# Hybrid decoder trunk: memory, x and norm weights also laid out features first, and the first layer's transposes replaced by loads

## The chip, the cores and the metric

The kernel runs on one core of a Trainium2 chip. The metric is the device time of one execution in microseconds (us). The kernel before was timed three times on the chip: 2645.34, 2647.21 and 2647.49 us, so its median is 2647.21 us. One more execution was taken with the hardware profiler; all views of the trace below are of that one.

## The reference

Four decoder layers act on x (256 rows of 2048 features, f32), with a memory of 256 rows of 2048 features. Cut to what matters here:

```python
mem_n = _rmsnorm(mem, mem_norm)
for i in range(DEPTH):                     # 4 layers
    h = _rmsnorm(x, norm_in[i])
    self_out, mq, gate = mixer_i(h)        # one of three causal mixers
    mem_out = _memory_attention(mq, mem_n @ w_mem_kv[i])
    y = concatenate([self_out, mem_out]) * silu(gate)
    x = x + y @ w_out[i]
return _rmsnorm(x, final_norm)
```

with `_rmsnorm(x, g) = x / sqrt(mean(x*x) + 1e-6) * g`. A product such as `mem_n @ w` sums over the 2048 features, so TensorE wants both operands with features on the partitions. The factor `1/sqrt(mean)` belongs to a row and can be applied to the product afterwards; the weight g belongs to a feature and is applied to the operand.

## The kernel before, in words

**Arithmetic.** Every f32 operand is split into two float32r parts, high and low: ScalarE copies the source into the high part (`split`, L60), VectorE subtracts it from the source to give the low part (L64). A product is the sum of high times high, high times low and low times high.

**Products.** `rows_by` (L222 on) makes 256 rows by up to 512 columns. It walks over the k tiles (128 features each) of a weight matrix in pairs. `stage` (L207) loads a pair (512 KB) on SyncE's queue (SP) into one of five buffers `wr`; `parts_of` splits one k tile into `wh` and `wl` (three buffers each); six matmuls of 128x512 follow (L234 to L236, for each half of the rows high times high, high times low, low times high). `columns_by` (L239 on) makes the transposed product, 256 columns at a time, four k tiles to a load (also 512 KB), each k tile with two pairs of matmuls (L253, 512 wide, and L255, 256 wide). The accumulators of both (`acc`) share four PSUM buffers, two to a call.

**Features first.** `to_features` (L182 on) takes 128 rows of 512 features, transposes four 128x128 blocks on TensorE into a PSUM tile (L186), multiplies by the norm weight of each feature on VectorE (L188) and splits the result (L60, L64). The norm weights come as rows (`vectors`, L78), are transposed on TensorE (`vectors_T`, L91) and lie in `gvec` with a feature on each partition.

**Order.** The program first prepares the memory for all four layers (`memory`, L307 on): for each of four chunks of 512 features it loads the memory's rows (`mrow`), makes `mT` by `to_features` and squares the rows for the mean (`square_sum`, L197: one ScalarE instruction and one that reads the accumulator). Then come a reduction, `rsqrt_mean` (twelve small VectorE instructions, L157 to L169) and `spread`, which lays the row factor along the columns through two small matmuls (L178). Then for layer i and half p_: one `rows_by` product "mv" (values), its scaling and store, and two `columns_by` products "mk" (keys, heads h). After the first mv product `late_constants` loads x and the other norm weights on SP, and after the first two mk products the four chunks of x go through `to_features` for layer 0 (`Norm.chunk`). The layers follow.

**What sets the order.** The kernel is traced in the order above and then planned: a list scheduler puts each engine's instructions into a fixed queue, ahead of their place in the program where its own timeline finds them ready and the engine free. `tc.keep_in_program_order` pins an instruction behind the one traced before it on its engine. A tile tag with `bufs=n` has n buffers, and a new tile waits for one to be released. Tag `pq` (five buffers of 4 KB a partition) holds the memory rows here, later the keys and queries. In the trace the planner has put the four loads of x, which the program has after the first product, at 9.96 us on SP's queue, and the transposes of x between the matmuls from 31.31 us on.

Of the kernel before, what the change touches and what calls it, by code (L numbers as in the profile page):

```python
# [8 lines left out]
F32 = mybir.dt.float32  # L9
# [22 lines left out]
def kernel(ctx: ExitStack, tc: tile.TileContext, a: dict, out: bass.AP,  # L32
# [39 lines left out]
    rows = cst.tile([P, P], F32, name="rows")  # L72
    mrow = []

    def vectors(src, o, n, eng):
        if len(src.shape) == 2:
            src = src.rearrange("l d -> (l d)")
        eng.dma_start(rows[o:o + n, :], src.rearrange("(r c) -> r c", c=P))  # L78

    def memory_rows(c):  # L80
        q = act.tile([P, 2, 512], F32, name="mrow", tag="pq", bufs=PQ)
        mrow.append(q)
        for t in range(2):
            eng = nc.scalar if t else nc.sync
            eng.dma_start(q[:, t, :], min_[t][:, c * 512:(c + 1) * 512])

    gvec = cst.tile([P, P], F32, name="gvec")

    def vectors_T(o, n):
        gp = misc("gp")  # L90
        nc.tensor.transpose(gp[:, :n], rows[o:o + n, :], ident[o:o + n, o:o + n])  # L91
        nc.vector.tensor_copy(gvec[:, o:o + n], gp[:, :n])
# [89 lines left out]
    def to_features(dst, t, src, gcol, n=4):  # L182
# [9 lines left out]
        g3 = xg[:, :n * P].rearrange("p (j c) -> p j c", j=n)  # L192
        split(dst[:, 0, :n, sl], dst[:, 1, :n, sl], g3)

    def square_sum(col, src):
        junk = tmp("junk")
        nc.scalar.activation(junk[:, :src.shape[-1]], src, AF.Square, accum_out=col)  # L197
# [21 lines left out]
        split(wh[:, :n], wl[:, :n], wr[:, c0:c0 + n])  # L219
        return wh, wl  # L220

    def rows_by(xt, kts, w, k0, cols, name):  # L222

        acc = [ps.tile([P, 512], F32, name=f"acc_{name}{t}", tag="acc", bufs=4) for t in range(2)]
        for s in range(0, kts, ST):
            m = min(ST, kts - s)
            wr, n = stage(w, k0 + s, m, cols)
            for k in range(m):
                wh, wl = parts_of(wr, k * n, n)
                q = xt[(s + k) // 4]  # L230
                for t in range(2):
                    xh, xl = (q[:, v, (s + k) % 4, t * P:(t + 1) * P] for v in range(2))
                    first, last = s + k == 0, s + k == kts - 1
                    nc.tensor.matmul(acc[t][:, :n], xh, wh[:, :n], start=first, stop=False)  # L234
                    nc.tensor.matmul(acc[t][:, :n], xh, wl[:, :n], start=False, stop=False)  # L235
                    nc.tensor.matmul(acc[t][:, :n], xl, wh[:, :n], start=False, stop=last)  # L236
# [37 lines left out]
    class Norm:  # L274
# [32 lines left out]
    def memory():  # L307
# [4 lines left out]
        mT = []  # L312
        for c in range(4):
            if c < 2:
                memory_rows(c + 2)
            q = act.tile([P, 2, 4, S], F32R, name="mT", tag=f"big{c}")
            mT.append(q)
            for t in range(2):
                to_features(q, t, mrow[c][:, t, :], c * 4)
                square_sum(mss[:, t * 4 + c:t * 4 + c + 1], mrow[c][:, t, :])  # L320
        s2 = small("ms2", 2)
        nc.vector.tensor_reduce(s2, mss.rearrange("p (t c) -> p t c", t=2), AX.X, OP.add)
        rsqrt_mean(mrstd, s2, D)
        nc.vector.tensor_scalar(m16, mrstd, 0.0625, None, op0=OP.mult)
        spread(mbc, m16)
        copies = [(v, g) for v in range(2) for g in range(4)]
        for i in range(depth):
            w = a["w_mem_kv"][i]
            for p_ in range(2):
                acc = rows_by(mT, 16, w, 0, (MEMW + p_ * 512, 512), "mv")  # L330
                v = [act.tile([P, 2, 512], F32R, name="mv", tag="aux", bufs=AUX) for z in range(2)]
                for t in range(2):
                    sc = mrstd[:, t:t + 1]
                    copy_act(v[0][:, t, :], acc[t], scale=sc)
                    nc.vector.scalar_tensor_tensor(v[1][:, t, :], acc[t], sc, f32(v[0])[:, t, :],
                                                   op0=OP.mult, op1=OP.subtract)
                for z in range(2):
                    nc.gpsimd.dma_start(mv[i][p_][:, z], v[z])
                if i == p_ == 0:
                    late_constants()  # L340
                for h in (2 * p_, 2 * p_ + 1):
                    acc = columns_by(mT, 16, w, 0, (h * 256, 256), "mk")
                    kT = act.tile([P, 2, 2, S], F32R, name="mkT", tag="pq", bufs=PQ)
                    for j in range(2):
                        z = total(acc[j])
                        zs = wk.tile([P, S], F32, name="zs", tag="z", bufs=3)
                        nc.vector.tensor_mul(zs, z, mbc)
                        split(kT[:, 0, j, :], kT[:, 1, j, :], zs)
                    nc.gpsimd.dma_start(mkT[i][h], kT)
                step = 2 * i + p_  # L350
                if step == 0:
                    for c in range(4):
# [500 lines left out]
def _constants():  # L853
# [18 lines left out]
            "c_cos": np.concatenate([c, c], 1), "c_sin": np.concatenate([-s, s], 1)}  # L872


_INS = ["x", "mem", "norm_in", "final_norm", "mem_norm", "rel_bias", "w_in_a", "a_q_norm", "w_uq",
        "a_kv_norm", "w_ukv", "w_in_b", "w_in_c", "c_sinks", "w_mem_kv", "w_out"]


# [19 lines left out]
```

## Time and profile before

| | before |
|---|---|
| median of 3 timed runs | 2647.21 us |
| the profiled execution's own time | 2644.4 us |
| its span, first to last instruction | 2642.5 us |
| TensorE matmul busy | 2614.7 us (99%) |
| VectorE busy | 1900.3 us (72%) |
| ScalarE busy | 1627.2 us (62%) |
| DMA moved | 507.51 MB, mean 192 GB/s |
| mean granted TensorE clock | 0.998 |

The profile page lists busy time by engine (PE is TensorE's matmuls, PEld its weight loads, DVE VectorE, ACT ScalarE, POOL GpSimd, SP SyncE), the chain of work that ended last, and groups of instructions by line. In a timeline row the first number is the start, the second the time that the merged instructions take, then engine, line, operation, output<-inputs, shapes and count; in brackets stands how long the engine sat idle before it and for whom. In a row of groups stand the busy sum in us, the mean ns of one instruction, and the idle time before. In a row of DMA issues stand the count, the size of one and the median us from issue to landing.

### The profile page before, as it was taken

What the parts mean: (1) busy time and instruction counts of PE and PEld (TensorE: products, weight loads), DVE (VectorE), ACT (ScalarE), POOL (GpSimd) and SP (SyncE); (2) the same over time, 40 slices, a digit from 0 to 9 for tenths busy, and PEclk for the clock granted to TensorE, in tenths of its full rate; (3) what the DMA queues carried; (4) which work ended last, traced back from release to release, by engine and by line L of the source; (5) the groups of instructions that cost most, each with busy time, mean ns of one, the idle gap of its engine ahead of it and who ended that gap; (6) DMA issues with size and microseconds to landing.
All of it is one profiled execution on the core that took longest, in us unless ns stands there. A gap on an engine that the chain in (4) does not pass through costs nothing.

```text
span 2642.5 us, 43005 instructions
## 1 busy us (share of the span) xinstructions
PE 2614.7 (99%) x14623; PEld 2268.1 (86%) x14623; DVE 1900.3 (72%) x4174; ACT 1627.2 (62%) x3460; POOL 57.8 (2%) x102
## 2 busy tenths in 40 slices
PE   8999999999999999999999999999999999999998
PEld 7788888888888888888888888888888888888886
DVE  7566656677777786877777776777778767777767
ACT  6455556566656566666666666666666656665555
POOL 1000000000000000000000000000000000000000
PEclk9999999999999999999999999999999999999999
DMA  7888887565557655555556565555555756655763
GB/s 266 273 269 270 278 262 209 160 191 161 171 164 216 191 191 168 170 184 173 172 166 193 189 191 177 169 175 180 189 166 164 203 163 188 165 170 153 224 184 134
DMA packets 454065, 507.51 MB, mean 192 GB/s; under 512 B 69300, under 2 KB 352180, under 8 KB 452692
## 3 DMA queue, kind: packets, MB, share of 16 engines
q1 hardware_dynamic: 439716, 446.42, 55.5%
q0 software_dynamic: 13120, 56.17, 6.7%
q8 instruction: 115, 1.88, 0.3%
q10 hardware_dynamic: 1008, 2.16, 0.2%
q14 instruction: 106, 0.87, 0.1%
HBM read 485.70 MB, written 31.56 MB: 196 GB/s over the span
## 4 chain that ended last, share of the span: by engine, by line
PE 97%; DMA 2%; DVE 1%; ACT 0%; issue 0%; ACTq 0%; POOLq 0%
PE acc_g L253 14%; PE acc_g L255 7%; PE acc_wo L234 7%; PE acc_wo L235 7%; PE acc_wo L236 7%; PE acc_mq L253 5%; PE acc_mk L253 5%; PE acc_qn L253 3%; PE acc_cq L253 3%; PE acc_mq L255 2%; PE acc_mk L255 2%; PE acc_q L234 2%; PE acc_q L235 2%; PE acc_q L236 2%; PE acc_mv L235 2%; PE acc_mv L234 2%
## 5 line engine op out<-in xcount | busy, mean ns | idle before, releaser
L64 DVE TENSOR_TENSOR wl<-wr,wh 128x512 fp32r<-128x512 f32 (+2 forms) x1776 | 1171.6, 663 | 609.7 <-ACT wh L60 577.7
L60 ACT ACTIVATE wh<-wr 128x512 fp32r<-128x512 f32 (+2 forms) x1776 | 1080.5, 609 | 809.6 <-PE acc_g L253 172.4
L253 PE MATMUL acc_g<-xT,wh 128*128 128x512 f32 x1536 | 518.8, 398 | 0.0
L255 PE MATMUL acc_g<-xT,wl 128*128 128x256 f32 x1536 | 374.2, 282 | 0.0
L255 PEld LDWEIGHTS acc_g<-xT,wl 128*128 128x128 f32 x1536 | 287.5, 189 | 28.0
L235 PE MATMUL acc_wo<-wl,y 128*128 128x512 f32 x768 | 303.6, 395 | 0.8 <-DVE wl L64 0.8
L236 PE MATMUL acc_wo<-wh,y 128*128 128x512 f32 x768 | 298.6, 390 | 0.0
L253 PEld LDWEIGHTS acc_g<-xT,wh 128*128 128x128 f32 x1536 | 265.2, 188 | 36.4
L234 PE MATMUL acc_wo<-wh,y 128*128 128x512 f32 x768 | 240.7, 393 | 0.6 <-ACT wh L60 0.6
L253 PE MATMUL acc_mq<-xT,wh 128*128 128x512 f32 x512 | 173.2, 397 | 0.0
L253 PE MATMUL acc_mk<-mT,wh 128*128 128x512 f32 x512 | 171.4, 397 | 0.0
L235 PEld LDWEIGHTS acc_wo<-wl,y 128*128 128x128 f32 x768 | 144.3, 188 | 29.7 <-DVE wl L64 1.6
L236 PEld LDWEIGHTS acc_wo<-wh,y 128*128 128x128 f32 x768 | 144.3, 188 | 27.9
L234 PEld LDWEIGHTS acc_wo<-wh,y 128*128 128x128 f32 x768 | 141.7, 188 | 28.9 <-ACT wh L60 0.8
L805 DVE TENSOR_TENSOR x<-x,acc_wo 128x512 f32<-128x512 f32 x192 | 126.2, 681 | 12.3 <-PE acc_wo L236 12.1
L253 PE MATMUL acc_qn<-cT,wh 128*128 128x512 f32 x384 | 129.6, 398 | 0.0
L253 PE MATMUL acc_cq<-xT,wh 128*128 128x512 f32 x384 | 127.8, 395 | 0.0
L255 PE MATMUL acc_mq<-xT,wl 128*128 128x256 f32 x512 | 126.5, 285 | 0.0
L255 PE MATMUL acc_mk<-mT,wl 128*128 128x256 f32 x512 | 123.0, 282 | 0.0
L255 PEld LDWEIGHTS acc_mk<-mT,wl 128*128 128x128 f32 x512 | 96.6, 189 | 10.8
L235 PE MATMUL acc_q<-wl,xT 128*128 128x512 f32 x256 | 102.4, 400 | 0.0
L235 PE MATMUL acc_mv<-wl,mT 128*128 128x512 f32 x256 | 100.8, 394 | 0.3 <-DVE wl L64 0.3
(284 smaller groups left out, 4533.9 us busy)
## 6 DMA issues: line engine op xcount, KB each, us to landing
wr<-in_w_out_dram SPq DMA_DIRECT2D x192, 512.0 KB, 3.7
wr<-in_w_in_a_dram SPq DMA_DIRECT2D x176, 512.0 KB, 3.8
wr<-in_w_mem_kv_dram SPq DMA_DIRECT2D x128, 512.0 KB, 4.7
wr<-in_w_in_b_dram SPq DMA_DIRECT2D x112, 512.0 KB, 3.4
wr<-in_w_in_c_dram SPq DMA_DIRECT2D x104, 512.0 KB, 3.5
wr<-in_w_uq_dram SPq DMA_DIRECT2D x288, 128.0 KB, 2.7
tab<-flat POOLq DMA_DIRECT2D x8, 1536.0 KB, 11.0
wr<-in_w_in_a_dram SPq DMA_DIRECT2D x32, 288.0 KB, 3.2
```

Source lines behind the costliest of these rows:

```text
L60: nc.scalar.activation(o, i, AF.Copy, scale=scale)
L64: nc.vector.tensor_sub(lo, src, f32(hi))
L234: nc.tensor.matmul(acc[t][:, :n], xh, wh[:, :n], start=first, stop=False)
L235: nc.tensor.matmul(acc[t][:, :n], xh, wl[:, :n], start=False, stop=False)
L236: nc.tensor.matmul(acc[t][:, :n], xl, wh[:, :n], start=False, stop=last)
L253: nc.tensor.matmul(acc[j], wh[:, o:o + P], q[:, :, kt % 4, :], start=first, stop=False)
L255: nc.tensor.matmul(acc[j][:, 0, :], wl[:, o:o + P], q[:, 0, kt % 4, :], start=False, stop=last)
L805: nc.vector.tensor_add(xs, xs, acc[t])
```

## The change

Three more arrays are given: `l_mem` and `l_x` (memory and x with a feature on each partition: 128 partitions x 16 blocks x 256 rows) and `l_norms` (all norm weights, one feature on each partition, 64 KB). `gvec` is loaded from `l_norms` by the first DMA on ScalarE's queue. The norm rows, their transposes and the copies are gone.

- The memory's features come in four chunks `ft` (two DMAs of 256 KB each, tag `pq`) on ScalarE's queue: two chunks ahead of everything, the other two asked for inside the first product. The first product calls `prepare(c)` before every fourth k tile, which makes chunk c of `mT` by `weighted_parts`: for each k tile ScalarE copies 128x256 with the weight as scale, and VectorE subtracts (one scalar_tensor_tensor of 128x256).
- The memory's rows are still loaded for the squares, all eight loads pinned on SP behind the weight loads of the first mk product (`row_scales`). The first mv product's scaling (`values`) now comes after that mk product and after `row_scales`.
- `late_constants` moves behind both mk products of the first step, and its four loads of x are pinned.
- For layer 0, `Norm.chunk` loads `l_x` (two DMAs of 256 KB for each of four chunks, on SP, not pinned, tag `pq`) and uses `weighted_parts` in place of `to_features`; the squares are still taken from x's rows. Layers 1 to 3 go on with `to_features`.

```diff
+    gvec = cst.tile([P, P], F32, name="gvec")
+    nc.scalar.dma_start(gvec, a["l_norms"])
+    def features(src, c, eng):
+        q = act.tile([P, 4, S], F32, name="ft", tag="pq", bufs=PQ)
+        for k in range(0, 4, 2):
+            eng.dma_start(q[:, k:k + 2, :], src[:, 4 * c + k:4 * c + k + 2, :])
+        return q
+    mft = [features(a["l_mem"], c, nc.scalar) for c in range(2)]
     ident = cst.tile([P, P], F32, name="ident")
     nc.scalar.dma_start(ident, a["c_ident"])
-    memory_rows(0)
-    vectors(a["mem_norm"], 0, 16, nc.gpsimd)
-    memory_rows(1)
-    vectors_T(0, 16)
...
-                nc.sync.dma_start(x[t][:, cs], xin[t][:, cs])
-        vectors(a["norm_in"], 64, 64, nc.sync)
-        vectors(a["a_q_norm"], 32, 24, nc.sync)
-        vectors(a["a_kv_norm"], 56, 8, nc.sync)
-        vectors_T(64, 64)
-        vectors_T(32, 32)
+                tc.keep_in_program_order(nc.sync.dma_start(x[t][:, cs], xin[t][:, cs]))
...
+    def weighted_parts(dst, src, gcol):
+        for k in range(4):
+            g = gvec[:, gcol + k:gcol + k + 1]
+            copy_act(dst[:, 0, k, :], src[:, k, :], scale=g)
+            nc.vector.scalar_tensor_tensor(dst[:, 1, k, :], src[:, k, :], g, f32(dst)[:, 0, k, :],
+                                           op0=OP.mult, op1=OP.subtract)
...
             wr, n = stage(w, k0 + s, m, cols)
+            if prepare is not None and s % 4 == 0:
+                prepare(s // 4)
...
+            if self.layer == 0:
+                weighted_parts(q, features(a["l_x"], c, nc.sync), 64 + c * 4)
             for t in range(2):
                 src = x[t][:, c * 512:(c + 1) * 512]
-                to_features(q, t, src, 64 + self.layer * 16 + c * 4)
+                if self.layer:
+                    to_features(q, t, src, 64 + self.layer * 16 + c * 4)
...
+        def prepare(c):
             if c < 2:
-                memory_rows(c + 2)
+                mft.append(features(a["l_mem"], c + 2, nc.scalar))
+            weighted_parts(mT[c], mft[c], c * 4)
+        def row_scales():
+            for c in range(4):
+                q = act.tile([P, 2, 512], F32, name="mrow", tag="pq", bufs=PQ)
+                for t in range(2):
+                    tc.keep_in_program_order(
+                        nc.sync.dma_start(q[:, t, :], min_[t][:, c * 512:(c + 1) * 512]))
+                    square_sum(mss[:, t * 4 + c:t * 4 + c + 1], q[:, t, :])
...
-                acc = rows_by(mT, 16, w, 0, (MEMW + p_ * 512, 512), "mv")
+                begins = i == p_ == 0
+                acc = rows_by(mT, 16, w, 0, (MEMW + p_ * 512, 512), "mv", prepare if begins else None)
+                if not begins:
+                    values(i, p_, acc)
+                for h in (2 * p_, 2 * p_ + 1):
+                    acck = columns_by(mT, 16, w, 0, (h * 256, 256), "mk")
+                    if begins and h == 0:
+                        row_scales()
+                        values(i, p_, acc)
+                    keys(i, h, acck)
+                if begins:
                     late_constants()
```

More of the change, by code (lines that the diff above doesn't have):

```diff
@@ L311, in memory @@
         mss = small("mss", 8, bufs=2)
-        mT = []
-        for c in range(4):
+        mT = [act.tile([P, 2, 4, S], F32R, name="mT", tag=f"big{c}") for c in range(4)]
+        def prepare(c):
             if c < 2:
-                memory_rows(c + 2)
-            q = act.tile([P, 2, 4, S], F32R, name="mT", tag=f"big{c}")
-            mT.append(q)
-            for t in range(2):
-                to_features(q, t, mrow[c][:, t, :], c * 4)
-                square_sum(mss[:, t * 4 + c:t * 4 + c + 1], mrow[c][:, t, :])
@@ new lines, in values @@
+        def values(i, p_, acc):
+            v = [act.tile([P, 2, 512], F32R, name="mv", tag="aux", bufs=AUX) for z in range(2)]
+            for t in range(2):
+                sc = mrstd[:, t:t + 1]
+                copy_act(v[0][:, t, :], acc[t], scale=sc)
+                nc.vector.scalar_tensor_tensor(v[1][:, t, :], acc[t], sc, f32(v[0])[:, t, :],
+                                               op0=OP.mult, op1=OP.subtract)
+            for z in range(2):
+                nc.gpsimd.dma_start(mv[i][p_][:, z], v[z])
@@ L326, in memory, with keys @@
+        def keys(i, h, acc):
+            kT = act.tile([P, 2, 2, S], F32R, name="mkT", tag="pq", bufs=PQ)
+            for j in range(2):
+                z = total(acc[j])
+                zs = wk.tile([P, S], F32, name="zs", tag="z", bufs=3)
+                nc.vector.tensor_mul(zs, z, mbc)
+                split(kT[:, 0, j, :], kT[:, 1, j, :], zs)
+            nc.gpsimd.dma_start(mkT[i][h], kT)
         copies = [(v, g) for v in range(2) for g in range(4)]
@@ L887 @@
     arrays, args = {}, {}
-    for name, v in [(n, inputs[n]) for n in _INS] + list(_constants().items()):
+    for name, v in ([(n, inputs[n]) for n in _INS] + list(_laid_out(inputs).items())
+                    + list(_constants().items())):
         v = _np.ascontiguousarray(v)
```

60 lines of the change are left out of this document (17 added, 43 removed).

## The prediction

> **What bounds the kernel now.** I read the page first: the busy sums, then the chain that ended last.
>
> ```profile
> PE 2614.7 (99%) x14623; PEld 2268.1 (86%) x14623; DVE 1900.3 (72%) x4174; ACT 1627.2 (62%) x3460; POOL 57.8 (2%) x102
> PE 97%; DMA 2%; DVE 1%; ACT 0%; issue 0%; ACTq 0%; POOLq 0%
> ```
>
> TensorE is the bound nearly everywhere: 97% of the chain is its matmuls. Work taken off it counts in full, and other engines' work counts only where TensorE waits. So next came the timeline of TensorE for the start, and two rows of the table by stage (us, PE, PEld, DVE, ACT, POOL busy, clock, DMA share, GB/s).
>
> ```profile
> 7.62 0.28 PE L91 MATMUL gp<-ident,rows 16*128 16x16 f32 x1 [7.62 <-DMA rows<-in_mem_norm_dram]
> 7.83 6.17 PE L186 MATMUL tp<-ident,mrow 128*128 128x128 f32 x32
> 14.31 0.73 PE L234 MATMUL acc_mv<-wh,mT 128*128 128x512 f32 x2 [0.31 <-ACT wh L60]
> ...
> 10.00:15.00 5.00, 4.69 (x26) 4.06 (x24) 5.00 (x9) 5.00 (x13) 0.00 (x0) 1.00 1.05 389
> 14.30:40.00 25.70, 25.35 (x121) 20.48 (x121) 22.54 (x52) 18.47 (x40) 0.00 (x0) 1.00 0.78 276
> ```
>
> The first product starts at 14.31: 7.62 us wait for a load of norm weights, then 32 transposes. From 14.30 to 40.00 TensorE idles 25.70 - 25.35 = 0.35 us. So the opening is as good as a product that starts at 14.66 and never waits. That opening, and the transposes of x later, are all that the change can win.
>
> **The change: transposes of x.** In the matmul timeline ten of them stand between two products, and the norm weights' two transposes stand just ahead of others.
>
> ```profile
> 30.93 0.45 PE L91 MATMUL gp<-ident,rows 64*128 64x64 f32 x2
> 35.70 1.25 PE L186 MATMUL tp<-ident,x 128*128 128x128 f32 x10
> 36.71 0.71 PE L234 MATMUL acc_mv<-wh,mT 128*128 128x512 f32 x2
> ...
> L186 PE MATMUL tp<-ident,x 128*128 128x128 f32 x32 | 4.8, 274 | 0.0
> ```
>
> Ten delay the next product from 35.70 to 36.71, 0.10 us each; the busy sum of the first 60 us, 4.8 us for 32, gives 0.15 each as an upper end. 32 x 0.11 = 3.6 us (3.2 to 4.8). The two norm transposes give 0.4. **Won: 4.0 us** (3.6 to 5.2), with no cover to lose, because TensorE has no slack here.
>
> **The change: when the first product starts.** It will need `gvec`, the first half of chunk 0, the first weights and one copy each on ScalarE. These landing times are of the first DMAs of before, in the view of DMA issues (the last two rows are for later).
>
> ```profile
> ident<-in_c_ident_dram ACTq DMA_DIRECT2D x1, 64.0 KB, 3.7
> mrow<-in_mem_dram SPq DMA_DIRECT2D x1, 256.0 KB, 5.4
> mrow<-in_mem_dram ACTq DMA_DIRECT2D x1, 256.0 KB, 7.1
> ...
> x<-in_x_dram SPq DMA_DIRECT2D x4, 512.0 KB, 9.5
> wr<-in_w_mem_kv_dram SPq DMA_DIRECT2D x1, 512.0 KB, 3.4
> ```
>
> The 64 KB on ScalarE's queue, issued at 0.73, landed at 4.4; `gvec` takes that place. SP's second 256 KB, issued at 1.2, landed at 6.6, which makes 512 KB on that queue: the first weights, now first there, should land then. On ScalarE's queue the second 256 KB, issued at 1.7, landed at 8.8. So the first half of chunk 0 comes near 6.6 and the second near 8.8. Then the copies:
>
> ```profile
> L188 DVE TENSOR_TENSOR xg<-tp,gvec 128x512 f32<-128x512 f32 x16 | 10.8, 684 | 1.4 <-PE tp L186 1.4
> L60 ACT ACTIVATE wh<-wr 128x512 fp32r<-128x512 f32 x32 | 20.0, 627 | 10.9 <-PE acc_mv L236 5.0 <-DVE wl L64 2.9 <-PE acc_mk L253 1.7
> L64 DVE TENSOR_TENSOR wl<-wr,wh 128x512 fp32r<-128x512 f32 x31 | 21.0, 685 | 2.9 <-ACT wh L60 2.6
> L64 DVE TENSOR_TENSOR mkT<-zs,mkT 128x256 fp32r<-128x256 f32 x2 | 0.8, 417 | 0.0
> L60 ACT ACTIVATE mkT<-zs 128x256 fp32r<-128x256 f32 x2 | 0.8, 402 | 0.0
> L335 DVE SCALAR_TENSOR_TENSOR mv<-acc_mv,mrstd,mv 128x512 fp32r<-128x512 f32 x2 | 1.5, 744 | 0.0
> L60 ACT ACTIVATE mv<-acc_mv,mrstd 128x512 fp32r<-128x512 f32 x2 | 1.3, 670 | 0.0
> ```
>
> If the planner lets the weights' copy in after the first feature copy, the start is 6.6 + 0.40 + 0.63 = 7.6. If all four feature copies stand ahead of it in ScalarE's queue, it waits for the second half: 8.8 + 2 x 0.40 + 0.63 = 10.2. I take **9.0**, about the middle, since nothing in the trace says which order the planner picks.
>
> Can the two copying engines feed it? Per four k tiles ScalarE does 4 x 0.40 + 4 x 0.63 = 4.1 us. For VectorE no row has a scalar_tensor_tensor of 128x256; it lies between the subtraction of 128x256 (0.417) and the one of 128x512 (0.744), and I take 0.44, near the row of its size: 4 x 0.44 + 4 x 0.685 = 4.5 us. Four k tiles are 24 matmuls, by the rows below 24 x 0.23 = 5.5 us. So TensorE stays the bound; at 0.744 VectorE would need 5.7 and the product would lose 0.8. The 32 subtractions and 32 copies replace 16 multiplications of 0.684 and 32 instructions of 128x512: VectorE has less to do, ScalarE 32 x 0.40 - 16 x 0.63 = 3 us more, off the path. DMA must bring 512 KB of weights and 256 KB of features per 2.7 us, 0.79 MB or 290 GB/s, under the 389 GB/s of the stage row. ScalarE issues ten DMAs instead of five at about 0.4 us each, before anything has landed.
>
> **The change: a slow clock.** The rows are mean durations at 9.6 to 10.6 us and 13.6 to 14.4 us, and the timeline of TensorE at full pace and after its one long wait.
>
> ```profile
> L186 PE MATMUL tp<-ident,mrow 128*128 128x128 f32 x6 | 1.5, 421 | 0.0
> L186 PE MATMUL tp<-ident,mrow 128*128 128x128 f32 x4 | 0.6, 272 | 0.0
> ...
> 18.51 0.39 PE L236 MATMUL acc_mv<-wh,mT 128*128 128x512 f32 x1
> 18.73 0.39 PE L235 MATMUL acc_mv<-wl,mT 128*128 128x512 f32 x1
> 132.78 1.22 PE L234 MATMUL acc_mv<-wh,mT 128*128 128x512 f32 x2 [2.87 <-ACT wh L60]
> 134.22 0.63 PE L236 MATMUL acc_mv<-wh,mT 128*128 128x512 f32 x1
> 134.65 0.63 PE L235 MATMUL acc_mv<-wl,mT 128*128 128x512 f32 x1
> ```
>
> The early transposes took 421 ns, the last 272, although the stage row shows a clock of 1.00: TensorE starts slow. After the wait at 132.78 matmuls follow each other in 0.43 us instead of 0.23, for some 2.7 us. Until now the transposes ran in the slow time, some 5 us; now the product does. Each slow microsecond loses 1 - 0.23/0.43 = 0.47: 1.3 (for 2.7 us) to 2.3 (for 5 us). I take **2.0**, nearer the row of the start. The Trainium skill ("TensorE: Matmul & The Clock Gate", Part 1) speaks against this change as well: it says that the array runs at half its clock until one activity window of about 3.4 us has been busy. By that page the loss would be an estimated 1.7 us, and the gain 0.3 us larger than by the rows.
>
> New opening: 9.0 + 2.0 + 0.35 of waits like before's = 11.35 against 14.66. **Won: 3.3 us.** The bounds: 14.66 - (7.6 + 1.3) = 5.8, and 14.66 - (11.5 + 2.3 + 0.7) = 0.2 with a second half that lands 1.3 us later than before's.
>
> **The change: a new wait.** The first mv product's two accumulators are held until `row_scales` has run, the first mk product takes the other two, so the second mk product waits for `values`. Queued behind it on TensorE is everything. Let E be the end of the first product, where the first mk matmul starts (39.94 before).
>
> ```profile
> 29.36 2.75 SPq L207 DMA_DIRECT2D wr<-in_w_mem_kv_dram  x2
> L197 ACT ACTIVATE junk<-mrow 128x512 f32<-128x512 f32 x8 | 4.9, 618 | 0.6 <-DMA mrow<-in_mem_dram 0.6
> L197 ACT ACTIVATION_READ_ACCUMULATOR junk<-mrow 128x1 f32 x8 | 1.5, 188 | 0.0
> ...
> 21.26 0.15 DVE L322 TENSOR_REDUCE ms<-mss 128x2 f32<-128x8 f32 x1
> 27.37 0.16 DVE L169 SCALAR_TENSOR_TENSOR mrstd<-rw,ry 128x2 f32<-128x2 f32 x1
> 39.94 0.72 PE L253 MATMUL acc_mk<-mT,wh 128*128 128x512 f32 x2
> 45.30 0.28 PE L255 MATMUL acc_mk<-mT,wl 128*128 128x256 f32 x1
> 45.65 0.27 PE L255 MATMUL acc_mk<-mT,wl 128*128 128x256 f32 x1
> ```
>
> The mk product takes 32 x 0.35 = 11.3 us. The second of the two loads at 29.36 is its last, issued by 32 us, E - 8; the eight memory rows are pinned behind it. They and that load are 2.6 MB, 6.7 us at 389 GB/s, plus 3.4 - 1.3 = 2.1 us that a lone 512 KB load takes beyond its bytes: landed at E + 0.8. The last chunk's squares take 2 x 0.81 = 1.6, reduction to factor 6.3, the scaling 2 x 0.67 + 2 x 0.74 = 2.8: released at E + 11.5, just as the second product wants them. I take **1.0 us lost** (0, to 5 by the third rival). SP's other additions, 2 MB of `l_x` and the pinned 2 MB of x, are not urgent; 2 MB is 5.4 us of DMA, and the weights behind them are wanted four loads of 2.8 us later, so I cost them at nothing; at 9.5 us of landing, as x before, they would cost up to 1.
>
> **Sum:** 4.0 + 3.3 - 1.0 = 6.3 us. The profiled execution would take 2644.4 - 6.3 = 2638.1; that execution is 2.8 us under the median of the timed runs, so I forecast 2647.2 - 6.3 = **2640.9**. About 0.2%, 5.3 us, is what a measurement of this kernel can tell from no change; the forecast lies just beyond it.
>
> **Rivals.**
> 1. *A later start eats it.* If all four feature copies stand first and the halves land late (start 11 to 11.5), 6.3 falls to about 4: 2643. For: five weight loads, 2.6 MB, now go out beside the features from the first microsecond on. Against: before's first DMAs shared the rate with as many others.
> 2. *Everything goes well.* Start 7.6, slow loss 1.3, transposes at 0.15, no wait: 5.8 + 5.2 = 11: 2636. Against: every term at its best.
> 3. *Slower: the row factors come too late.* The planner puts the squares where it believes the rows to have landed, and ScalarE's queue holds; x loads of before took 9.5 us to land on this queue, and `l_x`, not pinned, can take the `pq` buffers that the rows need. Release is at landing + 10.7, so the wait is landing - E - 0.6. With eight issues of 0.4 us and 9.5 us, rows land at E + 4.8: a wait of 4.2 plus 1.3 of slow clock, a gain of 1.8: 2645. With the four `l_x` chunks ahead, 4 x 0.44 us of VectorE each, 7.0 us more: a wait of 11.2, a loss of 5.2: 2652. The change is slower than before from a landing at E + 6.6 on, by 0.2% from E + 12. Against: the rows' loads stand ahead of `l_x` in the program.
> 4. *No change:* the opening wins nothing (0.2) and a wait of 4 us takes the transposes back: 2647. It needs 1 and 3 together.
>
> **Chances.** Forecast (gain 5.3 to 8.5) 0.40, rival 1 0.19, rival 2 0.16, rival 3 0.22 (half of it slower by over 0.2%), rival 4 0.03. Faster by over 0.2%: 0.40 + 0.16 = 0.56; slower 0.11; within 0.19 + 0.11 + 0.03 = 0.33. The range reaches rival 2 with 2 us for other placements by the planner, and the priced end of rival 3: 2634 to 2652.
>
> **What would show it.** In the profile after: no L186 with `x` in the first 100 us and no `gp` rows; the first `acc_mv` matmul at 9.0 (7.6 to 11.5) with durations near 0.63 for its first microseconds; TensorE's waits in the first product under 0.7; and before the second `acc_mk` a wait of 0 to 2 us. A wait there over 5, or ScalarE waiting for `mrow`, proves rival 3. The forecast is wrong if the later 2500 us, which the planner lays out anew, move by more than 2 us.

## The result and the profile after

Timed on one chip in turns, the changed kernel took 2652.27 us (median of 13 runs, 2649.38 to 2657.82) and the kernel before 2646.85 us (13 runs): a ratio of 1.0022, 95% interval [1.0014, 1.0029], so it is slower by some 4 to 8 us (5.4 between the medians). The forecast was 2641, with a range that ended at 2652. The profiled execution took 2652.68 us, with a span of 2650.7, 8.2 longer than before's 2642.5; the accounts below are of these two executions. Before's profiled execution lay 2.5 us under the median of its timed runs, which is most of the difference between 8.2 and 5.4.

The page's busy sums and the chain that ended last, after:

```profile
PE 2612.1 (99%) x14556; PEld 2262.5 (85%) x14556; DVE 1893.6 (71%) x4171; ACT 1631.5 (62%) x3476; POOL 57.3 (2%) x101
PE 96%; DMA 2%; DVE 1%; ACT 1%; SPq 0%; issue 0%; ACTq 0%; DVEq 0%
```

TensorE runs 67 matmuls fewer than before, which are the 64 transposes and three of norm weights, and is busy for 2.6 us less (2614.7 before). The span is longer all the same: the loss is waiting, and matmuls at a slow clock. To see where, I took the start of each product of the memory from the matmul timelines of both kernels (us from the start of the span):

| | before | after | gained (-) or lost since the row above |
|---|---|---|---|
| first mv product starts | 14.31 | 12.64 | -1.67 |
| first mk product starts | 39.94 | 37.10 | -1.17 |
| second mv product starts | 64.03 | 67.73 | +6.54 |
| its mk products start | 88.20 | 94.50 | +2.60 |
| third mv product starts | 110.70 | 116.99 | -0.01 |
| its mk products start | 137.03 | 144.56 | +1.24 |
| layer 0 starts | 381.5 | 388.7 | -0.3 |
| end of the span | 2642.5 | 2650.7 | +1.0 |

Nearly all is decided in the first 145 us. The row in which the second mv product starts understates its loss: two mk products that nothing holds up take 22.5 us (88.20 to 110.70 before, 94.50 to 116.99 after). Before's first two took 24.09, since 14 of the transposes of x stand between them, and after's took 30.63 without any, so 8.1 us were lost there.

The table by stage (us, then busy time of PE, PEld, DVE, ACT, POOL, granted clock, DMA share, GB/s) shows the same stretches, first of before (its first mk product ends near 52.8, inside the third row), then of after:

```profile
14.31:39.94 25.63, 25.29 (x121) 20.42 (x121) 22.47 (x51) 18.40 (x39) 0.00 (x0) 1.00 0.78 277
39.94:51.00 11.06, 11.06 (x70) 9.74 (x69) 11.06 (x21) 10.30 (x24) 4.67 (x8) 1.00 0.75 230
51.00:64.03 13.03, 13.03 (x77) 11.37 (x76) 10.07 (x32) 7.02 (x14) 1.05 (x2) 1.00 0.80 262
64.03:88.20 24.17, 24.17 (x106) 18.73 (x105) 14.55 (x28) 11.47 (x21) 3.10 (x6) 1.00 0.80 249
```

```profile
12.64:37.10 24.46, 24.46 (x97) 19.81 (x97) 16.98 (x32) 15.21 (x30) 0.00 (x0) 1.00 0.69 217
37.10:54.57 17.47, 13.55 (x69) 9.87 (x68) 10.15 (x29) 12.91 (x31) 0.00 (x0) 1.00 0.91 298
54.57:67.73 13.16, 13.16 (x65) 11.11 (x65) 9.17 (x29) 9.55 (x26) 3.18 (x6) 0.87 0.98 338
67.73:94.50 26.77, 24.80 (x107) 18.50 (x105) 20.54 (x45) 17.53 (x37) 5.65 (x10) 1.00 0.94 309
```

Before, TensorE never idles in the three later stretches. After, it idles 17.47 - 13.55 = 3.92 us in the first mk product and the gap behind it, and 26.77 - 24.80 = 1.97 in the second mv product, and the granted clock behind the first of these is 0.87. Three places need a closer look.

**The start.** The timeline of TensorE, then ScalarE's with its queue (ACTq rows are the DMAs that it issues):

```profile
12.64 1.22 PE L227 MATMUL acc_mv<-wh,mT 128*128 128x512 f32 x2 [12.64 <-ACT wh L60]
...
17.07 0.63 PE L228 MATMUL acc_mv<-wl,mT 128*128 128x512 f32 x1
17.50 0.54 PE L229 MATMUL acc_mv<-wh,mT 128*128 128x512 f32 x1
```

```profile
0.73 0.46 ACTq L73 DMA_DIRECT2D gvec<-in_l_norms_dram  x1
1.22 5.01 ACTq L79 DMA_DIRECT2D ft<-in_l_mem_dram  x4
8.13 0.33 ACTq L84 DMA_DIRECT2D ident<-in_c_ident_dram  x1
8.49 1.28 ACT L87 ACT_TABLE_LOAD   x1 [8.49 <-DMA wr<-in_w_mem_kv_dram]
8.56 0.38 ACTq L79 DMA_DIRECT2D ft<-in_l_mem_dram  x1
...
10.78 0.34 ACTq L79 DMA_DIRECT2D ft<-in_l_mem_dram  x1
11.16 0.51 ACT L60 ACTIVATE mT<-ft,gvec 128x256 fp32r<-128x256 f32 x1 [1.17 <-DMA wr<-in_w_mem_kv_dram]
```

The view of DMA issues has the landing of the first half of chunk 0:

```profile
ft<-in_l_mem_dram ACTq DMA_DIRECT2D x1, 256.0 KB, 6.6
```

It was issued at 1.22 and landed 6.6 us later, at 7.8. The first copy of it ran only at 11.16. In between, ScalarE stood at DMA issues. Most take 0.33 to 0.46 us, but they went out at 5.90 (the last of the four in the second row), 8.13, 8.56 and 10.78. Three of these times are those at which a weight load of SP's had landed (5.84, 8.13 and 10.76), and the trace names a weight load as what ScalarE waited for. ScalarE's compute is in the same queue and stood behind. TensorE's matmuls are slow from 12.64 to about 17.7.

**Between the two mk products.** SP's queue with the landing of the last of its loads, then ScalarE, VectorE and TensorE:

```profile
32.30 6.08 SPq L320 DMA_DIRECT2D mrow<-in_mem_dram  x8
...
mrow<-in_mem_dram SPq DMA_DIRECT2D x1, 256.0 KB, 6.4
```

```profile
37.57 0.63 ACT L187 ACTIVATE junk<-mrow 128x512 f32<-128x512 f32 x1 [2.36 <-DMA mrow<-in_mem_dram]
...
44.65 0.61 ACT L187 ACTIVATE junk<-mrow 128x512 f32<-128x512 f32 x1
...
52.43 0.63 ACT L187 ACTIVATE junk<-x 128x512 f32<-128x512 f32 x1 [1.22 <-DMA x<-in_x_dram]
...
53.06 1.24 ACT L60 ACTIVATE mv<-acc_mv,mrstd 128x512 fp32r<-128x512 f32 x2
```

```profile
45.39 0.16 DVE L323 TENSOR_REDUCE ms<-mss 128x2 f32<-128x8 f32 x1 [0.53 <-ACT junk L187]
...
50.64 0.16 DVE L151 SCALAR_TENSOR_TENSOR mrstd<-rw,ry 128x2 f32<-128x2 f32 x1
```

```profile
51.38 0.71 PE L160 MATMUL spr<-dg,ones 128*128 128x128 f32 x4 [0.72 <-DVE dg L159]
54.57 0.51 PE L246 MATMUL acc_mk<-mT,wh 128*128 128x512 f32 x1 [2.48 <-DVE mv L333]
...
55.40 0.63 PE L246 MATMUL acc_mk<-mT,wh 128*128 128x512 f32 x1
...
56.04 0.63 PE L246 MATMUL acc_mk<-mT,wh 128*128 128x512 f32 x1
```

The eight row loads went out over 6 us, because SP too stood at issues: the last was at issue from 36.9 to 38.4 and landed at 43.3, 6.4 us after 36.9. ScalarE waited 2.36 us for the first row, with copies of weights behind it, ran the eighth square at 44.65, and the factor was there at 50.8. Then the scaling, which frees the accumulators, stood behind a square of x that the planner had put ahead of it and whose row came 1.22 us late. TensorE waited 0.72 + 2.48 us, and 0.21 + 0.52 earlier in the product for weight copies: all of the 3.92. After it matmul pairs follow each other in 0.64 us (55.40 to 56.04) instead of 0.35, five times, which is 1.5 us. By the starts of the matmuls, with 11.25 us for an undisturbed mk product, the 8.1 us are 2.1 in the first one, 4.1 in the gap (0.71 of it the four `spr` matmuls, which stood in the first mv product before) and 1.9 in the second one.

**The second mv product.** ScalarE, then TensorE:

```profile
72.94 0.91 ACT L60 ACTIVATE xT<-ft,gvec 128x256 fp32r<-128x256 f32 x2 [1.29 <-DMA ft<-in_l_x_dram]
...
76.24 3.29 ACT L60 ACTIVATE xT<-ft,gvec 128x256 fp32r<-128x256 f32 x8
```

```profile
80.11 0.73 PE L227 MATMUL acc_mv<-wh,mT 128*128 128x512 f32 x2 [1.26 <-ACT wh L60]
81.55 0.50 PE L228 MATMUL acc_mv<-wl,mT 128*128 128x512 f32 x1 [0.71 <-DVE wl L64]
```

The sixteen feature copies of x come in a block; ScalarE waits for `ft` with them at the head of its queue, and TensorE runs out of weights. These two waits are the 1.97 us.

### The profile page after: what moved, and what is told of

It is laid out like the page before. It is cut to its first block, busy times and chain, and to the rows that moved or that the text cites. A ratio compares the mean times of both kernels' runs of the same rounds, so it can differ in the third digit from the quotient of the medians.

```text
span 2650.7 us, 42895 instructions
## 1 busy us (share of the span) xinstructions
PE 2612.1 (99%) x14556; PEld 2262.5 (85%) x14556; DVE 1893.6 (71%) x4171; ACT 1631.5 (62%) x3476; POOL 57.3 (2%) x101
## 4 chain that ended last, share of the span: by engine, by line
PE 96%; DMA 2%; DVE 1%; ACT 1%; SPq 0%; issue 0%; ACTq 0%; DVEq 0%
PE acc_g L246 14%; PE acc_g L248 7%; PE acc_wo L228 7%; PE acc_wo L227 7%; PE acc_wo L229 7%; PE acc_mq L246 5%; PE acc_mk L246 4%; PE acc_qn L246 3%; PE acc_cq L246 3%; PE acc_mq L248 2%; PE acc_q L227 2%; PE acc_q L228 2%; PE acc_q L229 2%; PE acc_mk L248 2%; PE acc_mv L228 2%; PE acc_mv L227 2%
## 5 line engine op out<-in xcount | busy, mean ns | idle before, releaser
L246 PEld LDWEIGHTS acc_mk<-mT,wh 128*128 128x128 f32 x512 | 89.2, 190 | 16.6 <-DVE mv L333 2.7
```

The costliest lines, as they stand in the source:

```text
L246: nc.tensor.matmul(acc[j], wh[:, o:o + P], q[:, :, kt % 4, :], start=first, stop=False)
```

## The experiments

**Theory Q (queues):** ScalarE and SP work in order, and the planner put DMA issues, squares and feature copies where it believes their data to be there; the data come later, and what is urgent stands behind. **Theory B (bandwidth), the rival:** the 4 MB more in the opening delay the weights themselves, whatever the order. Each of three sets of runs had a chip of its own and the kernel before beside it: at 2645.46 us for e1, e2, e3 and e5 (26 runs), at 2644.79 for e4, e6, e8 and e9 (33 runs), at 2644.58 for e10 to e12 (22 runs). Kernels of different sets are compared by their distance to that. The last columns are from the profiled executions: the start of the first product and of layer 0.

| kernel | median us | minus before | ratio to before, 95% interval | first product | layer 0 |
|---|---|---|---|---|---|
| before | 2646.85 | | | 14.31 | 381.5 |
| changed | 2652.27 | +5.4 | 1.0022 [1.0014, 1.0029] | 12.64 | 388.7 |
| e1: ScalarE issues fewer DMAs | 2651.76 | +6.3 | 1.0026 [1.0015, 1.0037] | 9.81 | 387.5 |
| e2: no memory rows | 2646.0 | +0.5 | 1.0002 [0.9993, 1.0011] | 12.5 | 380.6 |
| e3: x as before | 2652.47 | +7.0 | 1.0028 [1.0017, 1.0038] | 13.4 | 387.2 |
| e4: only x's part | 2644.73 | -0.1 | 0.9998 [0.999, 1.0007] | 14.09 | 378.6 |
| e5: rows ahead | 2646.36 | +0.9 | 1.0004 [0.9995, 1.0013] | 12.6 | 382.7 |
| e6: e1 and e5 | 2641.77 | -3.0 | 0.9990 [0.9981, 0.9999] | 9.44 | 378.0 |
| e8: e6, x spread | 2640.62 | -4.2 | 0.9984 [0.9975, 0.9993] | 10.59 | 376.2 |
| e9: e8, one table copy a step | 2640.07 | -4.7 | 0.9979 [0.997, 0.9987] | 9.65 | 371.5 |
| e10: before, one table copy a step | 2644.62 | 0.0 | 1.0002 [0.9993, 1.0011] | 14.47 | 376.5 |
| e11: changed, x's squares late | 2653.08 | +8.5 | 1.0031 [1.0019, 1.0044] | 13.22 | 389.3 |
| e12: e9, last copy earlier | 2640.01 | -4.6 | 0.9984 [0.9975, 0.9993] | 9.89 | 373.1 |

### e2_no_rows

```diff
-                q = act.tile([P, 2, 512], F32, name="mrow", tag="pq", bufs=PQ)
-                for t in range(2):
-                    tc.keep_in_program_order(
-                        nc.sync.dma_start(q[:, t, :], min_[t][:, c * 512:(c + 1) * 512]))
-                    square_sum(mss[:, t * 4 + c:t * 4 + c + 1], q[:, t, :])
+                nc.vector.memset(mss[:, 2 * c:2 * c + 2], 512.0)
```

> The changed kernel without the loads and squares of the memory's rows: the row factor comes from a constant, all else stays. Theory Q: the first mk product took 17.5 us in place of 11.3 because ScalarE stood before squares whose rows had not landed and the factor came late; now it takes 11.3 to 12 and the time falls by 5.5 to 6.5 us, to about 2646. Rival: x's squares, put ahead of the scaling, take the place of the wait, and only 3 us are won.

This kernel leaves out the loads and squares of the memory's rows and takes a constant for the row factor. Its time is that of before: 4.9 us of the changed kernel's 5.4 are gone (8.1 us at the start of layer 0), and TensorE's waits lost the row for `mv` and the one for `spr`. So the row factors account for most of what made the kernel slower. It leaves open whether it is the bytes or the order, since both went.

### e5_rows_early

```diff
+                if begins:
+                    row_scales()
+                    values(i, p_, acc)
                 for h in (2 * p_, 2 * p_ + 1):
                     acck = columns_by(mT, 16, w, 0, (h * 256, 256), "mk")
-                    if begins and h == 0:
-                        row_scales()
-                        values(i, p_, acc)
                     keys(i, h, acck)
```

> The changed kernel with the memory's rows, their squares and the scaling in front of the first mk product instead of behind it: the eight loads are pinned behind the last weight load of the first product, some 11 us earlier, where DMA stood nearly idle (73 GB/s at 20 to 25 us). Theory Q: no wait before the second mk product, the first takes 11.3 to 12 us, the time falls by 5 to 6.5 us, to 2646 to 2647. Theory B: the rows now hold up the weights of the mk products or the squares hold up the first product, and less than 3 us are won.

All bytes are still loaded; the rows only go out ahead of the first mk product's four weight loads instead of behind them, and the scaling comes ahead of that product. 4.5 of the 5.4 us are gone (6.0 at the start of layer 0), just under the 5 to 6.5 that Q expected. TensorE's waits in the whole span (us, times, longest):

```profile
PE acc_mv L227 <- ACT wh L60: 16.9, 4, 12.6
PE acc_kvb L227 <- ACT wh L60: 3.5, 1, 3.5
PE acc_mv L228 <- DVE wl L64: 1.2, 2, 1.0
PE acc_wo L228 <- DVE wl L64: 0.8, 2, 0.5
```

No row of `acc_mk` is left. The place is worth nearly as much as the whole of the rows, with the same bytes: Q, not B as it is put above, for this part. The new place also has more free DMA, so the run does not tell how much of the lateness was a late issue and how much a slow landing. There was room for the rows, as the changed kernel's row shows: from 20 to 25 us DMA ran at 73 GB/s.

```profile
20.00:25.00 5.00, 5.00 (x23) 3.96 (x22) 4.25 (x9) 3.41 (x7) 0.00 (x0) 1.00 0.28 73
```

### e1_act_free

```diff
-    mft = [features(a["l_mem"], c, nc.scalar) for c in range(2)]
+    mft = [features(a["l_mem"], c, nc.gpsimd if c else nc.scalar) for c in range(2)]
...
-    nc.scalar.dma_start(ident, a["c_ident"])
+    nc.gpsimd.dma_start(ident, a["c_ident"])
...
-                mft.append(features(a["l_mem"], c + 2, nc.scalar))
+                mft.append(features(a["l_mem"], c + 2, nc.gpsimd))
```

> The changed kernel with the identity and chunks 1 to 3 of the memory's features issued by GpSimd, so that ScalarE issues three DMAs in place of ten before its copies. Theory Q (queue order): ScalarE's copies stood behind DMA issues that had to wait for an earlier DMA (8.13, 8.56 and 10.78 us), while the data for the first matmul had landed by about 8 us. Then the first matmul comes at 8.5 to 9.5 us in place of 12.64, and the time falls by 3 to 4 us, to about 2648.5. Theory B (bandwidth): the data simply land late because 3.6 MB are under way at once. Then the first matmul stays at 11.5 or later and the time within 1 us of 2652.3.

The time is no better than the changed kernel's (+6.3 against +5.4, with overlapping intervals): a miss, though the start came as expected. TensorE's waits in the first 55 us:

```profile
9.81 0.80 PE L227 MATMUL acc_mv<-wh,mT 128*128 128x512 f32 x1 [9.81 <-ACT mT L60]
39.05 0.73 PE L246 MATMUL acc_mk<-mT,wh 128*128 128x512 f32 x2 [2.14 <-ACT wh L60]
49.14 0.71 PE L160 MATMUL spr<-dg,ones 128*128 128x128 f32 x4 [0.72 <-DVE dg L159]
52.38 0.80 PE L246 MATMUL acc_mk<-mT,wh 128*128 128x512 f32 x1 [2.53 <-DVE mv L333]
```

The first product starts 2.8 us and the first mk product 3.4 us earlier (33.74), and the first half of chunk 0 landed no sooner than in the changed kernel (8.0 against 7.8), so ScalarE's queue was what held the start. But the rows came no sooner by as much: a wait of 2.14 grew in the first mk product, and of the 3.4 us the second mk product kept 2.2 and layer 0 1.2, which the timed runs don't show. A gain ahead of a late arrival is given back at the arrival. What was left of the start is the landing of a load and again an order. ScalarE's rows, and the landing of the first features:

```profile
8.73 0.63 ACT L60 ACTIVATE wh<-wr 128x512 fp32r<-128x512 f32 x1 [1.71 <-DMA wr<-in_w_mem_kv_dram]
9.27 0.89 ACT L60 ACTIVATE mT<-ft,gvec 128x256 fp32r<-128x256 f32 x2
...
ft<-in_l_mem_dram ACTq DMA_DIRECT2D x1, 256.0 KB, 6.8
```

The features were there at 1.22 + 6.8 = 8.0, but a copy of weights stood ahead of theirs, and its load came at 8.7.

### e6_early_free

Both edits, e1 and e5, together.

> Both repairs in the changed kernel: GpSimd issues the identity and chunks 1 to 3 of the memory's features, and the memory's rows, squares and scaling stand in front of the first mk product. Theory Q: the start is at 9.8 us as with the first repair alone (which won 3.4 us by the end of the first product and gave 2.2 back in the wait before the second mk product), and with that wait gone it is kept: 2.5 to 3.5 us faster than the second repair alone, 2643 to 2644. Rival: the start's gain goes into any other wait (rows that land too late for the squares in the earlier product), 2645 or more.

3.0 us under before, the first version that is faster, if only just (the interval ends at 0.9999): 8.4 us won on the changed kernel, where e5 alone won 4.5 and e1 alone nothing that can be told. On e5 that is 3.9, somewhat more than Q expected. With the rows in time the earlier start is kept: layer 0 starts at 378.0, 4.7 us earlier than in e5.

### e3_x_as_before and e4_only_x

e3 is the changed kernel without `l_x` (layer 0 uses `to_features` as before); e4 is the kernel before with nothing but `l_x`.

```diff
-            if self.layer == 0:
-                weighted_parts(q, features(a["l_x"], c, nc.sync), 64 + c * 4)
...
-                if self.layer:
-                    to_features(q, t, src, 64 + self.layer * 16 + c * 4)
+                to_features(q, t, src, 64 + self.layer * 16 + c * 4)
```

> The changed kernel with layer 0's features again by transposes of x (no l_x loads). Theory Q: 32 transposes come back (3.6 us), and the runs of x copies that held the second mv product up go (2.6 us): about 1 us slower, 2653 (2651.5 to 2654.5). Theory B: 2 MB less to load ahead of the weights wins more than the transposes cost: 2650 or less.

> The kernel before with one part of the change: layer 0's features of x come from l_x without transposes; the memory is prepared as before. Theory Q: 3.6 us of transposes go, and bursts of x copies on ScalarE and VectorE that stand before the weights' copies cost some 2.6 us, as in the changed kernel's second mv product (26.8 us in place of 24.2): within 2 us of the kernel before, likely 1 faster. Theory B (the added 2 MB starve the weights): 2 us slower or more. If l_x cost nothing, as the prediction had it: 3.6 us faster.

Neither moved the time: e3 stands with the changed kernel (+7.0 against +5.4, the intervals overlap), e4 with before. In e3 the transposes are back and themselves wait 1.8 us for rows of x, while the second mv product no longer waits. In e4 the second mv product starts 3.6 us earlier than before (60.41 against 64.03), 0.2 of it from the first product's start: the other 3.4 are what the 32 transposes had cost. Then its second mv product takes 26.0 us against 24.17, so half of the gain is paid back there as it is scheduled. Layer 0 still starts 2.9 us earlier than before; the timed median shows none of it, and where the rest goes is not shown.

### e8_x_spread

e6 with one chunk of x's features in each of steps 1 to 4 of the memory, instead of four in a block in step 0.

```diff
-                    for c in range(4):
-                        nm.chunk(c)
-                    nm.finish()
...
+                if 1 <= step <= 4:
+                    nm.chunk(step - 1)
+                if step == 4:
+                    nm.finish()
```

> The kernel with both repairs, and the four l_x chunks taken one in each of the memory's steps 1 to 4 in place of all four together. Theory Q: the second mv product loses the burst of eight copies in a row and takes 24.2 us in place of 26.8: another 2 to 3 us, 2640.5 to 2642. Rival (the copies cost the same wherever they stand, or 0.5 MB more in each of the later steps starves the weights there): within 1 us of the kernel with both repairs.

The mk products of the second step start at 81.44 instead of 85.53, though the first product started 1.15 us later. The second mv product took 21.77 us instead of 28.24: its waits (1.72 us) went with the slow clock behind them, and some 2.4 us of small matmuls that stood in it (for bias tables and for x's row factors) stand elsewhere now. The third mv product took 1.5 us longer (27.20 against 25.68), since its wait of 3.38 has a slow clock behind it, which e6's wait of 3.35 there did not have. By layer 0 the gain is 1.8, and the medians differ by 1.15, which these intervals can't tell from nothing.

### e11_x_square_late

The changed kernel with x's squares and the rest of `Norm.finish` taken out of step 0 and put into step 2; the memory's rows as they were.

```diff
         def chunk(self, c):
...
-                square_sum(self.ss[:, t * 4 + c:t * 4 + c + 1], src)
+                if self.layer:
+                    square_sum(self.ss[:, t * 4 + c:t * 4 + c + 1], src)
         def finish(self):
+            if self.layer == 0:
+                for c in range(4):
+                    for t in range(2):
+                        square_sum(self.ss[:, t * 4 + c:t * 4 + c + 1], x[t][:, c * 512:(c + 1) * 512])
```

> The changed kernel, with the squares of x (and what hangs on them) moved from step 0 to step 2 of the memory; the squares of the memory's rows stay where they are. It splits the 2.48 us wait before the second mk product. Theory Q, that ScalarE's in-order queue is what counts: the scaling of the mv product no longer stands behind a square of x that waits 1.22 us for its row and runs 0.63, so the wait falls to 0.5 to 1, the slow clock behind it goes (1.5 us), layer 0 begins 2.5 to 4 us earlier than 388.7, and the time is 2648 to 2650 where the changed kernel measured 2652.3. Theory B, that the rows simply arrive late because four more megabytes are on the way: the chain from the last row's landing to the scaling is the same, the wait stays at 2 to 2.5, and the time within 1 us of 2652.

Neither theory's numbers came. ScalarE and TensorE:

```profile
38.52 0.63 ACT L187 ACTIVATE junk<-mrow 128x512 f32<-128x512 f32 x1 [2.85 <-DMA mrow<-in_mem_dram]
...
40.91 0.63 ACT L187 ACTIVATE junk<-mrow 128x512 f32<-128x512 f32 x1 [1.15 <-DMA mrow<-in_mem_dram]
```

```profile
39.81 0.73 PE L246 MATMUL acc_mk<-mT,wh 128*128 128x512 f32 x2 [0.70 <-ACT wh L60]
...
42.87 0.73 PE L246 MATMUL acc_mk<-mT,wh 128*128 128x512 f32 x2 [1.11 <-ACT wh L60]
...
87.32 1.22 PE L227 MATMUL acc_mv<-wh,mT 128*128 128x512 f32 x2 [2.73 <-ACT wh L60]
```

The wait ahead of the second mk product is gone, as Q has it, but that product starts at 54.4, hardly earlier than the changed kernel's 54.57: the first mk product began 0.45 us later, more time was lost behind the memory rows (0.70 + 1.11 us instead of 0.21 + 0.52), and two matmuls for a bias table (0.8 us) now stand in the gap. The slow clock there went, and the second mv product starts 1.1 us earlier (66.64), but in it a block of feature copies of x costs a wait of 2.73 with a slow clock behind it (a granted clock of 0.88 over that product), and the time is no better than the changed kernel's (+8.5, intervals overlapping). The square of x was only the last of several instructions in the way; taking one out moves the loss to the next.

### e9_spread_one_copy, e10_before_one_copy, e12_last_copy_early

All versions up to here have a wait in the third mv product (2.87 us before, 3.63 after), behind two copies of a 1.5 MB bias table that the program puts into step 1. e9 is e8 with one copy a step, e10 the kernel before with one copy a step, e12 is e9 with the last copy moved from step 7 to step 4.

```diff
-                for c in copies[:2 if step == 1 else 1]:
-                    table_copies(*c)
-                copies = copies[2 if step == 1 else 1:]
+                table_copies(*copies[0])
+                copies = copies[1:]
```

> The same with one table copy (1.5 MB read and written) in each memory step in place of two in the second: nothing is left out, the eighth copy comes one step later. Theory Q: the wait in the third mv product (3.6 us in the changed kernel, 2.9 in the one before) with its slow clock, some 4.5 us in all, is two copies side by side holding up the weights: 3 to 5 us faster than with both repairs and the spread, 2636 to 2638.5. Rival: one copy holds the weights up as well, and it is within 1.5 us.

> The kernel before, with one copy of a bias table (1.5 MB) after each memory step instead of two after step 1. It tells how much of the best kernel's gain belongs to the change. If the two copies of step 1 cause the 2.87 us wait in the mv product of step 2, that wait goes here as it went in e9 (from 3.38), TensorE's slow clock behind it too: layer 0 then begins 3 to 5 us earlier than before's 381.5, and the measured time falls by 0.5 to 4 us, 2641 to 2644.5, depending on what the copy that now stands last costs the product of layer 0 that waits for its weights (e9's 5.6 against 2 to 3.5 elsewhere). If the copies share nothing with that wait, time and wait stay. If it comes to 2640 or less, the change brings nothing even when repaired.

> e9 with the last table copy moved from step 7 to step 4, which then has two, so that none runs while layer 0's first weights are loaded. If the copy causes e9's 5.6 us wait in the second product of layer 0, the wait falls to 2 to 3.5 and the time to 2637 to 2639, unless the two copies of step 4 cost a wait of 2 to 4 us of their own in step 5, which would leave 2640. If the wait stays at 5 to 6, it belongs to the weight loads of layer 0 themselves (288 KB in rows under 2 KB).

The wait in the third mv product went in e9 and e10, so the two copies caused it. Another grew in its place, in layer 0's second product. The waits of e9, then of e10, then of e12:

```profile
PE acc_kvb L227 <- ACT wh L60: 5.6, 1, 5.6
```

```profile
PE acc_kvb L234 <- ACT wh L60: 6.0, 1, 6.0
```

```profile
PE acc_kvb L227 <- ACT wh L60: 2.9, 1, 2.9
PE acc_mv L227 <- ACT wh L60: 1.9, 2, 1.5
```

It is 2.3 before and 2.0 after. Without the last copy beside it (e12) it is back at 2.9, and TensorE waits in two mv products instead. The three are worth nothing in time: e10 equals before, e9 and e12 are within a microsecond of e8. So the gain of e9 belongs to the change with its repairs, not to the copies: 4.7 us under before, ratio 0.9979 [0.997, 0.9987].

## Why the prediction was wrong, step by step

- **TensorE bounds, the opening and the transposes are all there is to win: right.** No transposes of x (now L168) and no `gp` rows are left in the first 100 us, and e6, e8, e9 and e12 won 3 to 5 us on before.
- **Transposes of x, 4.0 won, and the slow clock, 2.0 lost: right, the second at the edge of its bounds.** e4, which drops nothing but the transposes of x, starts its second mv product 3.6 us earlier, 3.4 of it behind the first product's start, where 3.6 was forecast. In the changed kernel the first product took 24.46 us instead of 25.63. Its slow time was 5.1 us (12.64 to 17.7), so 0.47 x 5.1 = 2.4 was lost, just over the row-based bound of 2.3. The rule that the Trainium skill ("TensorE: Matmul & The Clock Gate", Part 1) states, full clock after at least one busy window of about 3.4 us, gave 1.7 with one window; here the measurement is longer, and it decides.
- **The start at 9.0: failed, and with it the bound of 11.5.** It was 12.64, a loss of 3.6 us. The step that failed is "ScalarE issues ten DMAs instead of five at about 0.4 us each, before anything has landed". The time of an issue that need not wait was right (0.33 to 0.46); that all go out at once was not. e1, with three of the ten left on ScalarE's queue, starts at 9.81. The landing estimate of 6.6 for the first half was low too (7.8).
- **The new wait, "1.0 us lost": failed; it was rival 3.** The two mk products took 8.1 us more than undisturbed ones (30.63 against 22.5), 3.92 of them idle. It lies between rival 3's two cases, beyond the nearer one (a wait of 4.2 and 1.3 of slow clock, 5.5 in all); its cause was named rightly (squares put where the rows are believed to be) and given 0.22. The step that failed is the landing of the rows, "landed at E + 0.8", which is 37.9 here: the last landed at 43.3, E + 6.2. Its terms were off in three places: the loads were first issued at E - 4.8 (32.30), not behind E - 8; SP's eight issues took 6.08 us; and the last landed 6.4 us after its issue began. From the last square on, the chain to the release came to 9.9 in the prediction (10.7 less one square of 0.81) and took 9.9 (44.65 to 54.57), of which 1.85 are the square of x with its wait, which I had not reckoned with; e11 shows that it was not the only one in the way.
- **`l_x` and the rows of x at nothing, "up to 1": failed.** 2.6 us in the second mv product. The prediction costed the DMA bytes here and had the copies as "3 us more, off the path". It did not ask where the sixteen of x would stand, which was ahead of weight copies in ScalarE's queue: 0.41 us each where they run back to back (3.29 us for eight), and 1.29 us of waiting for `ft`. e8 took the waits away by spreading them.
- **Feature copies at 0.40 us: low.** A group row of the changed kernel's first 60 us:

```profile
L60 ACT ACTIVATE mT<-ft,gvec 128x256 fp32r<-128x256 f32 x16 | 6.8, 494 | 1.2 <-DMA wr<-in_w_mem_kv_dram 1.2
```

  494 ns, not 402: the row that I took has no scale. The Trainium skill ("ScalarE: Activation LUTs", What ACT_TABLE_LOAD costs) has it: each operand that is a pointer to 128x1 adds about 93 ns, and this row agrees. Since the copies overlap, eight in 3.29 us, it cost little. VectorE's subtraction, taken at 0.44 us, took 0.48.
- **"The later 2500 us move by no more than 2": held behind layer 0 only.** From there to the end the span grew by 1.0. The third mv product had lost 1.24 by then, at the two table copies.

Of the transposes of x 18 stood in the first product and 14 behind it, so the forecast for the first product was -0.4 us and for the two mk products -0.5. By that the gap between forecast and profile, 6.3 + 8.2 = 14.5 us, is: start 3.6, first product -0.8, mk products 7.1, `l_x` 2.6, table copies 1.2, the end 1.0, less 0.3 elsewhere.

What stays open: whether the first loads can land sooner than the 8.0 us (features) and 8.7 us (second weight load) that held e1's start, how the lateness of the rows divides between late issue and slow landing, and how much of the wait in layer 0's second product belongs to its own loads. None of this was tried.

## What to carry to other kernels

A DMA issue on an engine that also computes is not free: ask what has landed when it comes up, and what stands behind it in that engine's queue. When work is moved later because it isn't urgent, find the first instruction in an in-order queue that needs its data, and check that nothing urgent stands behind that; here one place in the program (e5) was worth some 4.5 us, with the same bytes loaded. A gain at the start is only kept if the next late arrival does not wait for something else: two repairs gave 8.4 us together, and alone nothing that can be told and 4.5.

## What the runs showed of the hardware

- With more DMAs under way, an issue waits for an earlier DMA to land, and ScalarE's own work waits with it: eight DMAs of ScalarE and SP had been issued by 2.3 us, the ninth went out at 5.38, just after `gvec` had landed (5.33), and the tenth at 5.90, just after the first weights (5.84). ScalarE's next ones went out at 8.13, 8.56 and 10.78 us, and eight loads took SP 6.08 us to issue. The Trainium skill ("Trainium Kernel Development and Optimization", Key Constraints) says that issuing from several engines only saves the sequencer's issue time; here the engine that issued was worth 2.8 us of the first product's start (12.64 against 9.81), since that time held the waiting too.
- The length of a wait does not tell whether a slow clock follows. Behind the changed kernel's wait of 2.48 us matmul pairs stood 0.64 us apart for 3.2 us (55.40 to 58.60) instead of 0.35, some 1.5 us lost. In e6 a wait of 1.50 (before 74.56) had matmuls 0.43 us apart behind it instead of 0.23, up to about 77.5, while behind its wait of 3.35 (before 130.59) they stood 0.23 apart at once.
